# Sixteen instead of twelve contraction tiles of a down projection in a seven-product scheme

## The chip, the cores and the metric

The kernel runs on one core of a Trainium2 chip. The metric is the device time of one execution in microseconds; the time of a kernel is the median of several. Everything is computed in fp32. In this text PE is the matrix engine, PEld its weight loads, DVE the vector engine, ACT the scalar engine, POOL the GpSimd engine, and SP the engine that here only issues transfers.

## The reference

One layer of a hybrid encoder block on 512 tokens of 1024 channels. Shown is its frame; the three mixers (a bidirectional mLSTM, a neighbourhood attention and a cross attention) are left out, since the change does not touch them.

```python
def conv_glu_ffn(h, w_up, w_conv, b_conv, w_down):
    a, u = jnp.split(h @ w_up, 2, axis=-1)
    return (jax.nn.gelu(dwconv3(a, w_conv, b_conv)) * u) @ w_down

        x = x + merged @ w_out[l]
        x = x + conv_glu_ffn(rms_norm(x, ffn_norm_g[l]), w_ffn_up[l], w_ffn_conv[l], b_ffn_conv[l], w_ffn_down[l])
    return rms_norm(x, final_norm_g)
```

The last product, `@ w_down`, is the down projection: 512 tokens, a contraction over 2816 features, and 1024 columns out. Behind it come the residual sum and the final RMS norm.

## The kernel before

**Products.** Each fp32 operand is split into a high part (a rounded copy, formed by ACT) and a low part (the difference, formed by DVE). A product of two tiles is three matmuls into one sum: high by high, high by low, low by high (`mm3`, lines 195 to 198). A contraction tile is 128 features; a matmul takes a 128x128 block as its stationary side and streams 512 columns, or 256 near the end.

**The up projection.** For each of 22 feature tiles f two products run over the 8 tiles of the 1024 channels, `ua` and `uu`: 48 matmuls. Conv, gelu and the product with u follow on ACT and DVE while PE is in the next tile. The weights come through a ring of three raw buffers (`wr`, 512 KB each, SP's queue) and are split into rings of four tiles each (`wh`, `wl`; lines 178 and 179). The feature tiles f below 12 stay in fp32 (`uu_`), those from 12 on are split at once (`UH`, `UL`).

**The down projection by seven products.** Its first 2 * `WN` contraction tiles are done by the Strassen-Winograd scheme. Tokens are halved (256 each), so are the columns (512 each) and the contraction (`WN` tiles each). Instead of eight products of quarters there are seven, p1 to p7, each with `WN` tiles, 2 token tiles of 128 and 3 matmuls of 512 columns: 6 matmuls a tile. They need sums of quarters on both sides. The sums of the weights (T1 to T4) are formed by DVE under the up projection: `sum_load` (line 1254) loads four quarters of one tile as 1 MB into a buffer, four subtractions of 512 columns follow, and a store of 1 MB on POOL's queue puts them into `tdn`, a scratch in DRAM (line 1262). They are done three at a time, from f = 4 on. The sums of the tokens are formed by `ops_to` (line 1307) in front of each product, one half of a product's tiles (`GN` = `WN`/2) at a time: p5 takes a21 + a22 through a small scratch `s` (line 1325), p6 takes a22 - a21 after a21 has become a11 - a21 (lines 1334 and 1317), p3 takes a12 - a11 through the scratch (line 1327). The operand half is then split by ACT (line 1330) and DVE (line 1332) into a buffer of the pool `u`. The remaining `SN` contraction tiles are plain products: c0 for the left 512 columns, c1 for the right, 4 token tiles, 12 matmuls a tile.

**The order.** `SEGMENTS` gives the order of the products: p1, one tile of c0, p5, one of c0, p6, one of c0, p3, all of c1, two of c0, p7, p2, one of c0, p4, and at the end the last four tiles of c0. `raws_to`, `tiles_to` and `ops_to` load, split and form ahead by fixed distances: raw weights three pairs ahead, four split tiles, two or three operand halves. `todo` delays the additions of finished products by a few tiles. A scheduler puts the recorded instructions in order for each engine; each engine runs its list in order, and SP and POOL issue the transfers in order.

**Buffers.** The pool `u` has `NU` = 15 buffers of 2112 fp32 a partition. In the down projection five hold split u, four the fp32 u, two the residual with the half-done output, one the final norm's gain. Operand halves and every other pair of raw weights share the other three.

**The end.** The last four tiles of c0 are done token tile by token tile. A token tile's end is a sum with the residual (line 1499), a square with its sum on ACT (1418), a mean on DVE (1491), a power on POOL (1486), a scaling of the right half on ACT (1517) and of the left half on DVE (1518), and the store. The last token tile's four contraction tiles run in two halves of 256 columns, so that the first half's sum (1510) and square (1512) fall under the second; a small scalar (1515) carries the first half's square into the second's.

Of the kernel before, what the change touches and what calls it, by code (L numbers as in the profile page):

```python
# [11 lines left out]
F32 = mybir.dt.float32  # L12
# [93 lines left out]
def hybrid_block(ctx, tc, xg, xT, memT, wflat, wdn, wst, vecs, gbias, nabias, out):  # L106
# [1147 lines left out]
    def sum_load(k):  # L1254
# [5 lines left out]
        def store():  # L1260
# [3 lines left out]
        sums.extend([lambda: V.tensor_tensor(q[B11], q[B12], q[B11], op=ALU.subtract),  # L1264
                     lambda: V.tensor_tensor(q[B12], q[B22], q[B12], op=ALU.subtract),
# [16 lines left out]
    wraw, wsp, ops = {}, {}, {}  # L1282
    ahead = {"raw": 0, "tile": 0, "op": 0}
# [22 lines left out]

    def ops_to(n):
        while ahead["op"] < min(n, len(OPS)):
            name, g = OPS[ahead["op"]]
            v = [uu_[i][g][:, :GN * S].rearrange("p (k s) -> p k s", k=GN) for i in range(2)]  # L1310
            a11, a21, a12, a22 = v[0][:, :, :HS], v[0][:, :, HS:], v[1][:, :, :HS], v[1][:, :, HS:]
# [3 lines left out]
            srcs = [(0, GN, {"p1": a11, "p6": a11, "p7": a21, "p2": a12, "p4": a22}.get(name))]  # L1315
            if name == "p6":
                V.tensor_tensor(a11, a22, a21, op=ALU.subtract)
            elif srcs[0][2] is None:
                srcs = []
                for k in range(0, GN, 2):  # L1320
                    m = min(2, GN - k)
                    t = r3(scr(m * HS))
                    sl = slice(k, k + m)
                    if name == "p5":
                        V.tensor_tensor(t, a21[:, sl], a22[:, sl], op=ALU.add)
                    else:
                        V.tensor_tensor(t, a12[:, sl], a11[:, sl], op=ALU.subtract)
                    srcs.append((k, k + m, t))
            for i, j, src in srcs:
                A.activation(r3(h)[:, i:j], src, AF.Copy)  # L1330
            for i, j, src in srcs:
                V.tensor_tensor(r3(l)[:, i:j], src, r3(h)[:, i:j].bitcast(F32), op=ALU.subtract)
            if name == "p5":
                V.tensor_tensor(a21, a11, a21, op=ALU.subtract)
# [294 lines left out]
```

## Time and profile before

| | us |
|---|---|
| median of three runs (872.54 to 873.01) | 872.58 |
| profiled execution, its own time | 872.42 |
| its span in the trace | 870.6 |
| PE busy | 861.0 (99%) |
| DVE busy | 644.0 (74%) |
| ACT busy | 481.7 (55%) |
| first matmul of the down projection | at 747.08 |
| last matmul | at 862.72 |
| final operation on DVE | at 866.08 |

The granted clock of PE was 0.998 over the span. A row of a timeline gives the start, the duration, the engine, the line of the kernel, the operation with out<-in and the tile's shape; in brackets stands how long the engine had been idle before and what ended that. A name such as `wh` or `u` stands for all buffers of its ring; `at` and `mm` are sums in PSUM. Lines in the rows are those of the kernel before.

### The profile page before, as it was taken

The numbers are of one execution on the slowest core, as the hardware profiler recorded it, in microseconds if no ns is written. First come the engines' busy times: TensorE is split into PE (matmuls) and PEld (weight loads), VectorE is DVE, ScalarE is ACT, GpSimd is POOL, SyncE is SP. The second block draws the span as 40 slices with busy tenths as digits, with TensorE's granted clock in tenths as the row PEclk, the third lists the DMA queues.
The fourth block names the chain that finished last, engine by engine and source line by source line (L and its number), as shares of the span: only waits on it lengthen the run. The fifth ranks groups of instructions, "written<-read, shape, count | busy, mean of one in ns | idle before, by whom it ended". The sixth has DMA issues, their size and how long they took to land.

```text
span 870.6 us, 12096 instructions
## 1 busy us (share of the span) xinstructions
PE 861.0 (99%) x4176; PEld 723.3 (83%) x4176; DVE 644.0 (74%) x1365; ACT 481.7 (55%) x1003; POOL 87.2 (10%) x184
## 2 busy tenths in 40 slices
PE   9999999999999999999999999999999999999996
PEld 7898889888888888888888888888888888877885
DVE  7794698997477768897676659788667777984574
ACT  7563577764455658897534455444444444543353
POOL 0101100000343370600000000000000000000001
PEclk9999999999999999999999999999999999999999
DMA  8324642533343353533223434887222222456232
GB/s 276 100 75 147 196 141 85 173 107 112 96 132 88 107 145 112 159 119 122 97 97 110 145 109 145 292 288 242 80 97 99 96 98 95 154 167 218 61 120 97
DMA packets 43742, 117.50 MB, mean 135 GB/s; under 512 B 6041, under 2 KB 11161, under 8 KB 43681
## 3 DMA queue, kind: packets, MB, share of 16 engines
q1 hardware_dynamic: 34256, 103.73, 36.4%
q0 software_dynamic: 8992, 12.61, 5.3%
q8 instruction: 33, 0.54, 0.3%
q10 hardware_dynamic: 432, 0.39, 0.1%
q14 instruction: 29, 0.23, 0.1%
HBM read 106.20 MB, written 10.50 MB: 134 GB/s over the span
## 4 chain that ended last, share of the span: by engine, by line
PE 97%; DVE 1%; ACT 1%; issue 0%; DMA 0%; POOL 0%; POOLq 0%; ACTq 0%
PE mm L196 26%; PE mm L198 26%; PE mm L197 26%; PE at L197 4%; PE at L198 4%; PE at L196 4%; PE at L964 1%; PE at L945 1%; PE at L926 0%; PE at L927 0%; PE at L747 0%; PE at L795 0%; PE at L1052 0%; PE at L1244 0%; DVE u L1518 0%
## 5 line engine op out<-in xcount | busy, mean ns | idle before, releaser
L196 PE MATMUL mm<-u,wh 128*128 128x512 f32 (+1 forms) x907 | 353.6, 390 | 0.0
L198 PE MATMUL mm<-u,wl 128*128 128x512 f32 (+1 forms) x907 | 350.4, 387 | 0.0
L197 PE MATMUL mm<-u,wh 128*128 128x512 f32 (+1 forms) x907 | 350.1, 386 | 0.0
L178 ACT ACTIVATE wh<-wr 128x512 fp32r<-128x512 f32 (+1 forms) x256 | 159.9, 627 | 199.1 <-PE mm L197 158.2
L179 DVE TENSOR_TENSOR wl<-wr,wh 128x512 fp32r<-128x512 f32 (+2 forms) x258 | 175.5, 683 | 53.8 <-ACT wh L178 51.9
L198 PEld LDWEIGHTS mm<-u,wl 128*128 128x128 f32 x907 | 170.4, 188 | 34.7 <-DVE wl L179 0.2
L197 PEld LDWEIGHTS mm<-u,wh 128*128 128x128 f32 x907 | 170.7, 188 | 32.7
L196 PEld LDWEIGHTS mm<-u,wh 128*128 128x128 f32 x907 | 170.6, 188 | 32.8 <-ACT wh L178 0.4
L522 POOL DMA_DIRECT2D u<-nav_d x128 | 62.3, 511 | 70.6 <-DVE X L203 24.4
L197 PE MATMUL at<-wl,u 128*128 128x512 f32 (+2 forms) x172 | 60.0, 349 | 0.4 <-DVE wl L1303 0.3
L198 PE MATMUL at<-wh,u 128*128 128x512 f32 (+2 forms) x172 | 59.4, 346 | 0.0
L196 PE MATMUL at<-wh,u 128*128 128x512 f32 (+2 forms) x172 | 58.9, 348 | 0.4 <-ACT wh L1302 0.2
L197 PE MATMUL mm<-wl,u 128*128 128x512 f32 x108 | 42.2, 391 | 0.0
L198 PE MATMUL mm<-wh,u 128*128 128x512 f32 x108 | 42.1, 390 | 0.0
L196 PE MATMUL mm<-wh,u 128*128 128x512 f32 x108 | 41.6, 391 | 0.3 <-ACT wh L1302 0.3
L197 PEld LDWEIGHTS at<-wl,u 128*128 128x128 f32 x172 | 32.4, 188 | 6.2 <-DVE wl L1303 2.4
L196 PEld LDWEIGHTS at<-wh,u 128*128 128x128 f32 x172 | 32.1, 188 | 5.8 <-ACT wh L1302 2.1
L198 PEld LDWEIGHTS at<-wh,u 128*128 128x128 f32 x172 | 32.4, 189 | 3.8
L442 ACT ACTIVATE s<-pad,vec 128x512 f32<-128x512 f32 x30 | 24.4, 813 | 12.6 <-DVE pad L440 12.6
L1303 DVE TENSOR_TENSOR wl<-u,wh 128x512 fp32r<-128x512 f32 x30 | 20.1, 690 | 14.1 <-ACT wh L1302 14.0
L1302 ACT ACTIVATE wh<-u 128x512 fp32r<-128x512 f32 x30 | 18.2, 626 | 20.9 <-PE at L198 9.5
L1302 ACT ACTIVATE wh<-wr 128x512 fp32r<-128x512 f32 x32 | 19.6, 624 | 18.4 <-PE at L198 7.7
(338 smaller groups left out, 1126.6 us busy)
## 6 DMA issues: line engine op xcount, KB each, us to landing
wr<-wflat SPq DMA_DIRECT2D x125, 512.0 KB, 3.4
u<-wdn SPq DMA_DIRECT2D x6, 1024.0 KB, 7.6
tdn<-u POOLq DMA_DIRECT2D x6, 1024.0 KB, 5.5
nab<-nabias SPq DMA_DIRECT2D x16, 256.0 KB, 2.8
u<-nav_d POOLq DMA_DIRECT2D x128, 32.0 KB, 2.8
s<-xT SPq DMA_DIRECT2D x15, 256.0 KB, 3.8
u<-tdn SPq DMA_DIRECT2D x7, 512.0 KB, 3.9
wr<-wdn SPq DMA_DIRECT2D x5, 512.0 KB, 3.5
```

Source lines behind the costliest of these rows:

```text
L178: A.activation(h[:, u:v], src, AF.Copy)
L179: V.tensor_tensor(l[:, u:v], src, h[:, u:v].bitcast(F32), op=ALU.subtract)
L196: PE.matmul(ps, lh, rh, start=start, stop=False)
L197: PE.matmul(ps, lh, rl, start=False, stop=False)
L198: st["mm"] = PE.matmul(ps, ll, rh, start=False, stop=stop).ins
L442: A.activation(t1, pad[:, 0:512], AF.Identity, scale=vcol(w, i), bias=vcol(b, i))
L522: G.dma_start(vw[r * 32:(r + 1) * 32, i * 256:(i + 1) * 256], nav_v[hf, r, CW[b]:CW[b] + 32, hp * 256:(hp + 1) * 256])
L945: PE.transpose(pt[:, j * P:(j + 1) * P], sm[:, j * P:(j + 1) * P], ident)
L964: PE.matmul(py[:, bl * 256:(bl + 1) * 256], vw[:, c:c + P], pp[bl][:, hf * 256:(hf + 1) * 256], start=hf == 0, stop=hf == 1)
L1302: A.activation(h, src, AF.Copy)
L1303: V.tensor_tensor(l, src, h.bitcast(F32), op=ALU.subtract)
```

## The change

`WN` goes from 6 to 8, so that 16 of 22 contraction tiles go through the seven products and `SN` falls from 10 to 6. The rest follows from this or goes with it:

- The final segment of c0 is gone; p4 is the last. Its first two tiles run for both token tiles, the other six (`TK`) first for token tile 2 and then, in two halves of 256 columns, for token tile 3. The split weights of these six lie in three buffers of the pool `u` (`ends_w`) instead of the ring. Token tiles 0 and 1 are finished during p4 (`lead`, `finish`).
- Of the weight sums two subtractions of 512 columns become one of 1024. There are eight loads of 1 MB and eight stores instead of six.
- The token sums for p5 and p6 are formed in place by `early`, under the up projection, at f = 17 to 20, with the operand halves of p1 ahead of them. p3's two sums are formed in place in `ops_to`. No scratch is used, and the look-ahead is three halves throughout.
- The fp32 u still takes four buffers (now full), the split u three instead of five.

```diff
@@ -23,11 +23,10 @@
-WN = 6
+WN, TK = 8, 6
 SN = FT - 2 * WN
 SEGMENTS = (("p1", None), ("c0", (0,)), ("p5", None), ("c0", (1,)), ("p6", None), ("c0", (2,)), ("p3", None),
-            ("c1", range(SN)), ("c0", (3, 4)), ("p7", None), ("p2", None), ("c0", (5,)), ("p4", None),
-            ("c0", range(6, SN)))
+            ("c1", range(SN)), ("c0", (3, 4)), ("p7", None), ("p2", None), ("c0", (5,)), ("p4", None))
 NU = 15
@@ -1261,8 +1260,7 @@
-        sums.extend([lambda: V.tensor_tensor(q[B11], q[B12], q[B11], op=ALU.subtract),
-                     lambda: V.tensor_tensor(q[B12], q[B22], q[B12], op=ALU.subtract),
+        sums.extend([lambda: V.tensor_tensor(w[:, :2 * S], w[:, S:3 * S], w[:, :2 * S], op=ALU.subtract),
                      lambda: V.tensor_tensor(q[B22], q[B22], q[B11], op=ALU.subtract),
                      store])
@@ -1297,41 +1296,43 @@
             src = wraw.pop(TILES[ahead["tile"]])
-            h = wp.tile([P, HWT], F32R, tag="hi", name=nm("wh"), bufs=4)[:, :S]
-            l = wp.tile([P, HWT], F32R, tag="lo", name=nm("wl"), bufs=4)[:, :S]
+            i = ahead["tile"] - len(TILES) + TK
+            if i < 0:
+                h = wp.tile([P, HWT], F32R, tag="hi", name=nm("wh"), bufs=4)[:, :S]
+                l = wp.tile([P, HWT], F32R, tag="lo", name=nm("wl"), bufs=4)[:, :S]
+            else:
+                if i % 2 == 0:
+                    ends_w.append(unit(F32R))
+                h, l = [ends_w[-1][:, o * S:(o + 1) * S] for o in (i % 2, 2 + i % 2)]
...
+    def early(g, i):
+        a11, a21, a12, a22 = quarters(g)
+        if i == 0:
+            V.tensor_tensor(a21, a21, a22, op=ALU.add)
+        else:
+            V.tensor_tensor(a11, a21, a11, op=ALU.subtract)
...
-            srcs = [(0, GN, {"p1": a11, "p6": a11, "p7": a21, "p2": a12, "p4": a22}.get(name))]
-            if name == "p6":
-                V.tensor_tensor(a11, a22, a21, op=ALU.subtract)
-            elif srcs[0][2] is None:
-                srcs = []
-                for k in range(0, GN, 2):
-                    m = min(2, GN - k)
-                    t = r3(scr(m * HS))
-                    sl = slice(k, k + m)
-                    if name == "p5":
-                        V.tensor_tensor(t, a21[:, sl], a22[:, sl], op=ALU.add)
-                    else:
-                        V.tensor_tensor(t, a12[:, sl], a11[:, sl], op=ALU.subtract)
-                    srcs.append((k, k + m, t))
-            for i, j, src in srcs:
-                A.activation(r3(h)[:, i:j], src, AF.Copy)
-            for i, j, src in srcs:
-                V.tensor_tensor(r3(l)[:, i:j], src, r3(h)[:, i:j].bitcast(F32), op=ALU.subtract)
-            if name == "p5":
-                V.tensor_tensor(a21, a11, a21, op=ALU.subtract)
+            if name == "p3":
+                V.tensor_tensor(a21, a22, a11, op=ALU.subtract)
+                V.tensor_tensor(a11, a12, a11, op=ALU.subtract)
+            src = {"p1": a11, "p5": a21, "p6": a11, "p3": a11, "p7": a21, "p2": a12, "p4": a22}[name]
+            A.activation(r3(h), src, AF.Copy)
+            V.tensor_tensor(r3(l), src, r3(h).bitcast(F32), op=ALU.subtract)
@@ -1388,8 +1389,14 @@
-        if f == FT - 4:
-            ops_to(1)
+        i = f - 2 * WN
+        if 1 <= i < 5:
+            g = (i - 1) // 2
+            if i % 2:
+                ops_to(g + 1)
+                early(g, 0)
+            else:
+                early(g, 1)
@@ -1440,87 +1446,95 @@
+    def lead(t):
+        V.tensor_tensor(xt[t][:, :S], A4[t], xt[t][:, :S], op=ALU.add)
+        squares(t, part[t], 0, S)
+
+    def finish(t):
+        x, col = xt[t], power(mean(part[t]))
+        A.activation(x[:, S:], x[:, S:], AF.Copy, scale=col)
+        V.scalar_tensor_tensor(x[:, :S], x[:, :S], col, gfin[:, :S], op0=ALU.mult, op1=ALU.mult)
+        SY.dma_start(out[t * P:(t + 1) * P, :], x)
...
             if ks is None and k % GN == 0:
-                ops_to(OPS.index((name, k // GN)) + (2 if j == 0 else 3))
+                ops_to(OPS.index((name, k // GN)) + 3)
...
+            if name == "p4":
+                if k < WN - TK:
+                    for t in range(2):
+                        wino(name, A4[2:], k, t, full, False, t == 1 and k == WN - TK - 1)
...
+                    plain(name, k, t, A4[t], full, k == 0, t < 2 and k == SN - 1)
+                if k == SN - 1:
+                    later(2, lambda: (lead(0), lead(1)))
+                    later(4, lambda: (finish(0), finish(1)))
+
+    x = xt[3]
+    V.tensor_tensor(x[:, :S], A4[3], x[:, :S], op=ALU.add)
+    tk = range(WN - TK, WN)
+    for k in tk:
+        wino("p4", A4[2:], k, 0, full, False, k == WN - 1)
+    lead(2)
+    z, ends = unit(), [atps(), atps()]
+    for e in range(2):
+        cs = slice(e * HS, (e + 1) * HS)
+        for k in tk:
+            wino("p4", [None, ends[e][:, :HS]], k, 1, cs, k == tk[0], k == WN - 1)
+        if e == 0:
+            finish(2)
+        V.tensor_tensor(z[:, cs], ends[e][:, :HS], x[:, cs], op=ALU.add)
...
```

Up to the feed-forward stage the instructions stand as before on every engine. In the following rows a name's last number tells the buffers apart. First ACT around the operand halves of p6; before, `u_1420_7610` and `u_1432_7654` are these two halves, and the `wh` rows between them are splits of weight tiles:

```order
L1330 ACTIVATE u_1406_7548<-s_1408_7551 128x256
L1302 ACTIVATE wh_1417_7592<-wr_1411_7568 128x512
L1408 ACTIVATE s_1431_7645<-at_1397_7509 128x512
L1302 ACTIVATE wh_1421_7614<-wr_1411_7568 128x512
L1330 ACTIVATE u_1420_7610<-u_1048_5547 128x768
L1302 ACTIVATE wh_1425_7626<-u_1416_7590 128x512
L1302 ACTIVATE wh_1428_7638<-u_1416_7590 128x512
L1302 ACTIVATE wh_1433_7658<-wr_1419_7608 128x512
L1330 ACTIVATE u_1432_7654<-u_1098_5818 128x768
L1302 ACTIVATE wh_1436_7670<-u_1427_7636 128x512
```

And with the change, where they are `u_1421_7618` and `u_1436_7673`:

```order
L1334 ACTIVATE u_1421_7618<-u_1048_5547 128x1024
L1415 ACTIVATE s_1432_7652<-at_1398_7512 128x512
L1307 ACTIVATE wh_1422_7621<-u_1412_7576 128x512
L1307 ACTIVATE wh_1426_7633<-wr_1417_7598 128x512
L1307 ACTIVATE wh_1429_7645<-wr_1417_7598 128x512
L1307 ACTIVATE wh_1433_7661<-u_1420_7616 128x512
L1334 ACTIVATE u_1436_7673<-u_1114_5908 128x1024
L1307 ACTIVATE wh_1437_7676<-u_1420_7616 128x512
```

A half is now 1024 columns wide and comes with four weight tiles' splits between it and the next one instead of three. Second, DVE under the up projection of f = 17 with the change, where neither of the two wide rows stood before (L178 splits a weight tile of the up projection, L1335 is the low part of an operand half of p1, L1321 the first sum in place):

```order
L178 TENSOR_TENSOR wl_1322_7109<-wr_1306_7022,wh_1321_7108 128x512
L1335 TENSOR_TENSOR u_1326_7144<-u_1048_5547,u_1326_7144 128x1024
L439 TENSOR_TENSOR pad1_140<-mm_1317_7070,rb_2_5625 128x512
L178 TENSOR_TENSOR wl_1324_7113<-wr_1306_7022,wh_1323_7112 128x512
L1321 TENSOR_TENSOR u_1048_5547<-u_1048_5547 128x4x256
L442 SCALAR_TENSOR_TENSOR s_1318_7096<-pad1_140,vec_78,s_1318_7096 128x512
L178 TENSOR_TENSOR wl_1330_7152<-wr_1312_7060,wh_1329_7151 128x512
```

Each wide row stands between two rows that PE's weight loads or the conv depend on. Third, the end on DVE, before and with the change (`at` of 256 columns are the two halves of the last token tile, and `u_1384_7487` or `u_1385_7490` is the final gain):

```order
L1499 TENSOR_TENSOR u_1047_5545<-mm_1387_7491,u_1047_5545 128x512
L1510 TENSOR_TENSOR u_1597_8430<-at_1583_8359,u_1047_5545 128x256
L1491 TENSOR_SCALAR y_1595_8423<-y_1560_8258,y_1593_8420 128x1
L1518 SCALAR_TENSOR_TENSOR u_1047_5545<-u_1047_5545,y_1596_8425,u_1384_7487 128x512
L1491 TENSOR_SCALAR y_1600_8447<-y_1562_8262,y_1598_8444 128x1
L1510 TENSOR_TENSOR u_1597_8430<-at_1584_8360,u_1047_5545 128x256
L1515 SCALAR_TENSOR_TENSOR u_1597_8430<-y_1600_8447,y_1601_8449 128x1
L1518 SCALAR_TENSOR_TENSOR u_1047_5545<-u_1597_8430,y_1604_8468,u_1384_7487 128x512
```

```order
L1515 TENSOR_TENSOR u_1047_5545<-mm_1389_7495,u_1047_5545 128x512
L1461 TENSOR_TENSOR u_1047_5545<-mm_1388_7494,u_1047_5545 128x512
L1457 TENSOR_SCALAR y_1594_8421<-y_1567_8276,y_1589_8397 128x1
L1467 SCALAR_TENSOR_TENSOR u_1047_5545<-u_1047_5545,y_1595_8423,u_1385_7490 128x512
L1527 TENSOR_TENSOR u_1591_8400<-at_1592_8401,u_1047_5545 128x256
L1457 TENSOR_SCALAR y_1598_8432<-y_1569_8280,y_1596_8429 128x1
L1532 SCALAR_TENSOR_TENSOR u_1591_8400<-y_1598_8432,y_1599_8434 128x1
L1527 TENSOR_TENSOR u_1591_8400<-at_1593_8402,u_1047_5545 128x256
L1535 SCALAR_TENSOR_TENSOR u_1047_5545<-u_1591_8400,y_1602_8459,u_1385_7490 128x512
```

The scaling of the token tile before (L1518, now L1467) stood between the two halves' sums and now stands ahead of both; the small scalar (L1515, now L1532) stood behind the second sum and now stands ahead of it.

More of the change, by code (lines that the diff above doesn't have):

```diff
@@ L1426, in half_done, with wino @@
             V.tensor_tensor(xt[t][:, S:], xt[t][:, S:], gfin[:, S:], op=ALU.mult)
-    def wino(name, ps, k, start, stop):
+    def wino(name, ps, k, t, cs, start, stop):
         g, kk = divmod(k, GN)
@@ L1431, in wino @@
         wh, wl = wsp[name, k]
-        for t in range(2):
-            q = slice(kk * HS + t * P, kk * HS + (t + 1) * P)
-            mm3(ps[t], h[:, q], l[:, q], wh, wl, start, stop or t == 1 and name == "p4" and k == WN - 1)
+        q = slice(kk * HS + t * P, kk * HS + (t + 1) * P)
+        mm3(ps[t], h[:, q], l[:, q], wh[:, cs], wl[:, cs], start, stop)
     def plain(name, k, t, ps, cs, start, stop):
@@ new lines, in hybrid_block @@
+    x = xt[3]
[12 more added lines that the diff above has]
+        V.tensor_tensor(z[:, cs], ends[e][:, :HS], x[:, cs], op=ALU.add)
+        v = tiny(1)
+        A.activation(scr(HS + e), z[:, e * HS:(e + 1) * HS + e], AF.Square, scale=D ** -0.5, accum_out=v)
+        if e == 0:
+            v = mean((part[3][0], v))
+            V.scalar_tensor_tensor(z[:, S:S + 1], v, D ** 0.5, power(v), op0=ALU.mult, op1=ALU.mult)
```

110 lines of the change are left out of this document (41 added, 69 removed).

## The prediction

> **What bounds the kernel now.** I read the page first, then the chain of waits, then TensorE by stages, and last the waits inside the stage that the change rewrites.
>
> ```profile
> span 870.6 us, 12096 instructions
> PE 861.0 (99%) x4176; PEld 723.3 (83%) x4176; DVE 644.0 (74%) x1365; ACT 481.7 (55%) x1003; POOL 87.2 (10%) x184
> PE 97%; DVE 1%; ACT 1%; issue 0%; DMA 0%; POOL 0%; POOLq 0%; ACTq 0%
> ```
>
> TensorE (PE) is the bound: busy in 99% of the span, 97% of the chain. A change can then act in three ways: the number of matmuls, the gaps between them, and the end behind the last. For the first I need the distance between starts, from PE's timeline (start, duration; a duration overlaps the next start):
>
> ```profile
> 719.88 0.39 PE L196 MATMUL mm<-u,wh 128*128 128x512 f32 x1
> ...
> 723.28 0.39 PE L196 MATMUL mm<-u,wh 128*128 128x512 f32 x1
> ...
> 747.08 0.39 PE L196 MATMUL at<-wh,u 128*128 128x512 f32 x1
> ...
> 859.97 0.28 PE L196 MATMUL at<-wh,u 128*128 128x256 f32 x1
> ...
> 862.72 0.28 PE L198 MATMUL at<-wh,u 128*128 128x256 f32 x1
> ```
>
> Between the first two rows lie 15 steps: 3.40/15 = 0.2267 us for 512 columns. Between the last two lie 23: 2.75/23 = 0.1196 us for 256. The down projection begins at 747.08 and its stream ends at 862.72 + 0.12 = 862.84, after 115.76 us. The order counts 480 matmuls of 512 columns and 24 of 256 in it: 480 x 0.2267 + 24 x 0.1196 = 111.68. So **4.08 us** of this stage are gaps. Busy time by stretches says where (columns: PE, PEld, DVE, ACT, POOL, clock, DMA share, GB/s):
>
> ```profile
> 747.08:755.24 8.16, 8.16 (x38) 6.76 (x37) 8.16 (x15) 6.51 (x12) 0.00 (x0) 1.00 0.55 169
> 755.24:791.00 35.76, 34.61 (x141) 25.43 (x140) 30.69 (x51) 17.56 (x32) 0.00 (x0) 1.00 0.53 160
> 791.00:855.00 64.00, 64.00 (x284) 53.00 (x284) 36.31 (x55) 26.33 (x45) 0.00 (x0) 1.00 0.36 117
> ```
>
> Only 755 to 791 shows idle PE (1.15 us; in the rest of the 4.08 PE counts as busy, since a matmul's duration covers part of each gap). That is the run through p5, p6 and p3. The table of waits (total, times, longest) for ACT from 747 to 792 and for the weight loads:
>
> ```profile
> ACT u L1330 <- PE at L198: 15.3, 5, 3.6
> PEld at L197 <- DVE wl L1303: 2.4, 5, 0.8
> PEld at L196 <- ACT wh L1302: 2.1, 4, 0.6
> ```
>
> PE's weight loads wait for wh and wl, the split weight tiles. Why these are late stands in one piece of the timelines:
>
> ```profile
> 756.17 0.96 DVE L1334 TENSOR_TENSOR u<-u 128x768 f32<-128x768 f32 x1
> 756.31 0.19 PEld L197 LDWEIGHTS mm<-wl,u 128*128 128x128 f32 x1 [0.43 <-DVE wl L1303]
> 762.68 0.85 ACT L1330 ACTIVATE u<-u 128x768 fp32r<-128x768 f32 x1 [3.58 <-PE at L198]
> 763.43 1.13 ACT L1302 ACTIVATE wh<-u 128x512 fp32r<-128x512 f32 x2
> 764.09 0.30 PEld L196 LDWEIGHTS at<-wh,u 128*128 128x128 f32 x2 [0.52 <-ACT wh L1302]
> ```
>
> There are two causes. First, at 762.68 the copy of an operand half (L1330) has stood 3.58 us at the head of ACT's queue, until PE was done with the half whose buffer it takes; behind it, at 763.43, stands the split of the next weight tile, which PE needs six matmuls = 1.36 us after the release. That pattern comes five times. Second, up to 756 DVE is full with the sums of tokens (8.16 of 8.16 us in the first stretch), and wl waits behind them.
>
> **The change part by part.** *Matmuls.* The order has 462 + 36 now, 18 long ones fewer and 12 short ones more: -18 x 0.2267 + 12 x 0.1196 = **-2.64 us**. The Trainium skill (TensorE: Matmul & The Clock Gate, "Back-to-back issue gap") gives N/2.4 + 2.5 ns for an isolated matmul, 215.8 and 109.2 ns here; by it the term were -2.57. The rows decide.
>
> *Gaps.* Of the 15 buffers of this pool, three were left for operand halves and raw weights (12 hold the up projection's result, the residual and a gain); now five are. In the new order the halves of p6 and p3 take buffers whose last reader is done by the time that the ring of four split tiles lets ACT go on anyway; one, the second half of p6, still waits for the end of p5's first half, but the tile behind it is due 18 matmuls = 4.1 us later instead of 1.36. The p5 and p6 sums leave this stage. What remains costs, by these rows (out<-in, count, busy, mean ns, idle):
>
> ```profile
> L1303 DVE TENSOR_TENSOR wl<-u,wh 128x512 fp32r<-128x512 f32 x30 | 20.1, 690 | 14.1 <-ACT wh L1302 14.0
> L1330 ACT ACTIVATE u<-u 128x768 fp32r<-128x768 f32 x10 | 8.4, 843 | 12.1 <-PE at L198 9.6 <-DVE wl L1303 2.3
> L1332 DVE TENSOR_TENSOR u<-u,u 128x768 fp32r<-128x768 f32 x10 | 9.6, 958 | 5.7 <-ACT u L1330 5.5
> ```
>
> 256 columns more cost DVE 958 - 690 = 268 ns, so 1024 columns are 1.23 us (an estimate, like the next figures). A half of four weight tiles is 24 matmuls = 5.44 us of PE against 4 x 0.69 + 1.23 = 3.99 us of DVE. From p1 to the end of p3 the order puts 49 instructions of 512 and 11 of 1024 columns on DVE: 49 x 0.69 + 11 x 1.23 = 47.3 us at most against 228 matmuls = 51.7 us, 92%; before, 8.16 + 30.69 = 38.85 of 43.92, 88%. That is no lighter; but the sums now stand where nothing waits for them. Walking the rows of DVE and ACT with these durations (a successor starts about 0.1 before the listed end), each weight tile is ready a microsecond or more ahead, tightest at p5's last tile. Bounds: all gaps go, **-4.08**, or all stay, 0. I take -4.08, since both causes are removed by name, and keep 0 for the range.
>
> *Up projection.* One 1 MB load, one 1 MB store and four 512-wide subtractions come for each of two more tiles; at f = 17 and 19 one operand half and a sum (two 1024-wide, 2.5 us), at f = 18 and 20 one sum. The rows for single feature tiles, and the stores:
>
> ```profile
> 559.37:570.73 11.36, 11.36 (x55) 9.41 (x53) 11.36 (x20) 4.76 (x8) 1.08 (x2) 1.00 0.82 292
> 570.73:582.10 11.37, 11.37 (x55) 9.41 (x53) 10.88 (x18) 5.51 (x9) 1.21 (x2) 1.00 0.90 320
> 627.10:638.00 10.90, 10.90 (x50) 9.04 (x49) 7.38 (x11) 4.61 (x8) 0.00 (x0) 1.00 0.31 96
> L1262 POOL DMA_DIRECT2D tdn<-u x6: 752/753/797, 547.9 to 600.1; - x6
> ```
>
> PE did not idle with DVE full for a whole tile, nor at 320 GB/s. Each tile with a sum now moves 3 x 1.05 MB in 11.36 us = 277 GB/s, no more than was seen, over two tiles more. At f = 17 DVE has 7.38 + 2.5 = 9.9 of 10.9 us. So I take **0** under this cover; uncovered, the eight subtractions (4.8 us at the listed pace of 0.60 each) and the six pieces of 1024 columns (6 x 1.23 = 7.4) would cost up to 12 us. The Trainium skill (SBUF — State Buffer, "Who interferes with whom") says that a DVE operation with two SBUF inputs contends with GpSimd's reads, and that descriptors of a queue that GpSimd writes can starve. That speaks against two more stores on POOL's queue under such subtractions; but the stores' rows read 752 to 797 ns beside a full DVE, so the trace shows no holding, and I leave the term at 0.
>
> *End.* The rows of DVE and ACT behind the last long matmuls:
>
> ```profile
> 854.73 0.69 DVE L1499 TENSOR_TENSOR u<-mm,u 128x512 f32<-128x512 f32 x1 [1.36 <-PE mm L198]
> 857.11 0.75 DVE L1518 SCALAR_TENSOR_TENSOR u<-u,y,u 128x512 f32<-128x512 f32 x1 [0.69 <-POOL y L1486]
> 857.78 0.68 DVE L1499 TENSOR_TENSOR u<-mm,u 128x512 f32<-128x512 f32 x1
> 861.60 0.42 DVE L1510 TENSOR_TENSOR u<-at,u 128x256 f32<-128x256 f32 x1
> 862.46 0.19 ACT L1512 ACTIVATION_READ_ACCUMULATOR s<-u 128x1 f32 x1
> 863.14 0.75 DVE L1518 SCALAR_TENSOR_TENSOR u<-u,y,u 128x512 f32<-128x512 f32 x1 [0.65 <-POOL y L1486]
> 863.81 0.21 DVE L1491 TENSOR_SCALAR y<-y,y 128x1 f32<-128x1 f32 x1
> 863.94 0.42 DVE L1510 TENSOR_TENSOR u<-at,u 128x256 f32<-128x256 f32 x1
> 864.67 0.16 DVE L1515 SCALAR_TENSOR_TENSOR u<-y,y 128x1 f32<-128x1 f32 x1 [0.32 <-POOL y L1486]
> 864.92 0.42 ACT L1512 ACTIVATE s<-u 128x257 f32<-128x257 f32 x1 [1.06 <-DVE u L1515]
> 866.08 0.75 DVE L1518 SCALAR_TENSOR_TENSOR u<-u,y,u 128x512 f32<-128x512 f32 x1 [1.25 <-POOL y L1486]
> ```
>
> Now the final operation of the last token tile starts 866.08 - 862.84 = 3.24 us behind the stream. One reason: the last matmul's record ends at 862.72 + 0.28 = 863.00, but its sum starts at 863.94, because DVE first finishes the token tile before (863.14) and a mean (863.81). In the new order the halves last 36 x 0.1196 = 4.31 us from a point T, so more of the tile before falls under them. With steps from the rows: sum of that tile at about T + 0.2 (estimate: a record runs 0.16 past the next start), its last operation 857.11 - 854.73 = 2.38 later, first half's sum 857.78 - 857.11 = 0.67 later (T + 3.25), its square summed at 862.65 - 861.60 = 1.05 later (T + 4.30), the scalar of L1515 864.67 - 863.81 = 0.86 later (T + 5.16), second half's sum 0.13 later (T + 5.29), its square 0.46 later, the final operation 866.08 - 864.92 = 1.16 later: T + 6.91, 2.60 us behind the stream. **-0.64 us**; at best the second sum waits for nothing and the final operation comes 0.16 + 0.46 + 1.16 = 1.78 behind (-1.46), at worst nothing is won (0).
>
> *Sum*, against the profiled execution's own 872.42 us (median of the runs 872.58): 872.42 - 2.64 - 4.08 - 0.64 = **865.06**, say 865.1.
>
> **The rivals.** *The gaps stay.* For it: DVE is as full as before in this run (92% by the high durations), p6's second half still waits, and p5's last tile has only a microsecond. Against it: the queue behind each wait is now long. A step that is later than my walk by over 1 us decides. All gaps kept give 872.42 - 2.64 - 0.64 = 869.1, half of them 867.1.
>
> *Transfers become the bound, and it is slower.* Seven products need a new 0.262 MB weight tile each six matmuls: 0.262 MB/1.36 us = 193 GB/s, and the stretch of products is longer now. These rows bear on it (a window, and the issue of one load with its time to landing):
>
> ```profile
> 790.00:800.00 10.00, 10.00 (x46) 8.27 (x45) 4.87 (x8) 3.27 (x5) 0.00 (x0) 1.00 0.88 290
> u<-tdn SPq DMA_DIRECT2D x7, 512.0 KB, 3.9
> ```
>
> One load at a time would be 0.524 MB/3.9 us = 134 GB/s, and 755 to 791 ran at 160. If 160 were a limit, the 35 tiles up to p3's end (9.17 MB) would take 57.3 instead of 51.7 us, and the 25 of p7, p2, p4 and c0 (6.55 MB) 41.0 instead of 35.4: +11.2, so 865.1 + 11.2 = 876.3. It is slower than before once the rate stays under 15.72 MB/(87.1 + 7.4 us) = 166 GB/s. Against it: 290 GB/s in 790 to 800 with PE full, and the low rate of 160 stood where PE itself was waiting for ACT and DVE.
>
> *The up projection shows what it hides.* If each of the eight tiles with sums overran by the added 0.6 us of DVE: 8 x 0.6 = 4.8, 869.9. Against it: only two of these tiles filled DVE, and the weights are three loads ahead.
>
> That the change does not do what it says is out: the order has six matmuls fewer and the sums where they should be.
>
> **How the numbers follow.** Forecast (864.0 to 866.2) 0.62; gaps stay, half or more, 0.22; up projection 0.05; transfers 0.06, a third of it mild and still faster; something else 0.05, either way. The range reaches over the kept gaps: 863.9 to 869.2, leaving out about 0.15. What tells from no change is 0.2%, 1.7 us. Faster takes the first three cases, the mild transfers and half of the rest: 0.62 + 0.22 + 0.05 + 0.02 + 0.02 = 0.93, cut to 0.92; same 0.03; slower 0.05.
>
> **What would show it.** In the new profile: 462 and 36 matmuls from about 747 on, ending 109.04 us later (462 x 0.2267 + 36 x 0.1196), with PE's share of each stretch at its full width; the weight loads' waits for wh and wl at L1307 and L1308 under 0.5 us in sum; the waits of L1334 for PE shorter; the down projection's start still at 747.1, else the up projection has paid; the final operation some 2.6 us behind the last matmul. Waits of L1307 for a DMA would speak for the transfers, waits of weight loads for wl alone for a DVE that is too full. A time above 869.2 would make my walk of the rows wrong, one above 872 the whole reading.

## The result and the profile after

The changed kernel takes 865.38 us in the median (865.00 to 865.74) against 872.62 us; the ratio is 0.9916, with an interval of 0.9899 to 0.9933. The profiled execution took 865.0 us, 7.42 us less than the one before, and the page of the changed kernel reads (first lines, and the chain by engine):

```profile
span 863.2 us, 12105 instructions
PE 855.3 (99%) x4170; PEld 722.1 (84%) x4170; DVE 653.6 (76%) x1359; ACT 487.2 (56%) x1001; POOL 88.8 (10%) x186
...
PE 99%; DVE 0%; ACT 0%; POOL 0%; POOLq 0%; issue 0%
```

PE is still the bound, and the chain now has hardly anything else in it. The down projection on PE's timeline, its first matmul, the first of the 36 halves and the last:

```profile
746.88 0.39 PE L195 MATMUL at<-wh,u 128*128 128x512 f32 x1
...
851.60 0.28 PE L195 MATMUL at<-u,u 128*128 128x256 f32 x1
...
855.79 0.28 PE L197 MATMUL at<-u,u 128*128 128x256 f32 x1
```

From 746.88 to 855.79 + 0.12 = 855.91 are 109.03 us. The matmuls alone are 462 x 0.2267 + 36 x 0.1196 = 109.04. Nothing is left for gaps, and the table of waits for the weight loads is empty from 440 us on. The busy time by stretches shows the same, with DVE as full as before or fuller and with more transfer (PE, PEld, DVE, ACT, POOL, clock, DMA share, GB/s):

```profile
747.00:755.00 8.00, 8.00 (x37) 6.64 (x36) 8.00 (x13) 5.59 (x9) 0.00 (x0) 1.00 0.66 197
755.00:791.00 36.00, 36.00 (x160) 29.80 (x160) 30.80 (x44) 21.29 (x32) 0.00 (x0) 1.00 0.65 206
791.00:852.00 61.00, 61.00 (x273) 50.55 (x272) 41.30 (x63) 30.30 (x54) 1.10 (x2) 1.00 0.42 135
```

ACT still waits for PE, but in small pieces, and at another instruction (the two largest rows for it from 747 to 792, and the one for an operand half):

```profile
ACT wh L1307 <- PE at L197: 10.1, 15, 0.7
ACT wh L1307 <- PE mm L197: 2.8, 3, 1.1
...
ACT u L1334 <- PE at L197: 0.7, 1, 0.7
```

Fifteen times it is the weight split itself that waits for its ring of four, which is what a loop that runs ahead looks like; an operand half waits once for PE, for 0.7 instead of five times for 15.3 us in sum. The end on DVE:

```profile
851.80 0.69 DVE L1461 TENSOR_TENSOR u<-mm,u 128x512 f32<-128x512 f32 x1 [2.61 <-PE mm L197]
...
854.15 0.75 DVE L1467 SCALAR_TENSOR_TENSOR u<-u,y,u 128x512 f32<-128x512 f32 x1 [0.65 <-POOL y L1452]
854.81 0.42 DVE L1527 TENSOR_TENSOR u<-at,u 128x256 f32<-128x256 f32 x1
...
856.67 0.16 DVE L1532 SCALAR_TENSOR_TENSOR u<-y,y 128x1 f32<-128x1 f32 x1 [0.65 <-POOL y L1452]
856.75 0.42 DVE L1527 TENSOR_TENSOR u<-at,u 128x256 f32<-128x256 f32 x1
858.43 0.75 DVE L1535 SCALAR_TENSOR_TENSOR u<-u,y,u 128x512 f32<-128x512 f32 x1 [1.26 <-POOL y L1452]
```

The final operation starts 858.43 - 855.91 = 2.52 us behind the stream, before 3.24. So the 7.42 us come from the stage's length (115.76 to 109.03: -6.73), its end (-0.72), a start that is 0.20 earlier, a stretch behind the final operation that is 0.25 longer (4.52 to 4.77 us), and 0.02 outside the span. The start lies between 746.88 and 747.65 in all runs here that leave the mixers' buffers alone, so the 0.20 is no effect of the change that I could claim.

### The profile page after: what moved, and what is told of

Its sections match the earlier page's. It is cut to its first block, busy times and chain, and to the rows that moved or that the text cites. A ratio compares the mean times of both kernels' runs of the same rounds, so it can differ in the third digit from the quotient of the medians.

```text
span 863.2 us, 12105 instructions
## 1 busy us (share of the span) xinstructions
PE 855.3 (99%) x4170; PEld 722.1 (84%) x4170; DVE 653.6 (76%) x1359; ACT 487.2 (56%) x1001; POOL 88.8 (10%) x186
## 4 chain that ended last, share of the span: by engine, by line
PE 99%; DVE 0%; ACT 0%; POOL 0%; POOLq 0%; issue 0%
PE mm L195 26%; PE mm L197 26%; PE mm L196 26%; PE at L195 5%; PE at L197 5%; PE at L196 5%; PE at L963 1%; PE at L944 1%; PE at L925 0%; PE at L926 0%; PE at L746 0%; PE at L794 0%; PE at L1243 0%; PE at L1051 0%; PE at L224 0%; PE mm L403 0%
## 5 line engine op out<-in xcount | busy, mean ns | idle before, releaser
L178 DVE TENSOR_TENSOR wl<-wr,wh 128x512 fp32r<-128x512 f32 (+2 forms) x258 | 175.6, 684 | 56.9 <-ACT wh L177 54.9
L197 PE MATMUL mm<-wh,u 128*128 128x512 f32 x92 | 35.8, 389 | 0.0
L196 PE MATMUL mm<-wl,u 128*128 128x512 f32 x92 | 35.8, 389 | 0.0
L195 PE MATMUL mm<-wh,u 128*128 128x512 f32 x92 | 35.7, 389 | 0.0
L1261 POOL DMA_DIRECT2D tdn<-u x8 | 6.1, 762 | 252.5 <-DVE u L1260 252.5
L1308 DVE TENSOR_TENSOR wl<-wr,wh 128x512 fp32r<-128x512 f32 x34 | 23.2, 689 | 8.8 <-ACT wh L1307 8.7
```

The costliest lines, as they stand in the source:

```text
L178: V.tensor_tensor(l[:, u:v], src, h[:, u:v].bitcast(F32), op=ALU.subtract)
L195: PE.matmul(ps, lh, rh, start=start, stop=False)
L196: PE.matmul(ps, lh, rl, start=False, stop=False)
L197: st["mm"] = PE.matmul(ps, ll, rh, start=False, stop=stop).ins
L1261: G.dma_start(tdn[:, :, k * S:(k + 1) * S].rearrange("q p n -> p q n"), w4)
L1308: V.tensor_tensor(l, src, h.bitcast(F32), op=ALU.subtract)
```

## The experiments

The question was no longer how much, but why the gaps went. The prediction named two causes: too few free buffers for operand halves, and sums of tokens that fill DVE in the down projection. In the following, the length of the stream is read from PE's timeline as above, and its gaps are that length less the matmuls at 0.2267 and 0.1196 us. "Late" and "early" say where the sums stand in the program. Where DVE ran them is another matter, since the scheduler orders the instructions: "in the stage" counts, by the trace, how many of the four sums (two halves of p5, two of p6) DVE ran with the down projection and not under the up projection. Through the scratch the first of them starts 0.27 us ahead of the stage's first matmul and is counted.

| kernel | tiles | free buffers | sums for p5, p6 | in the stage | stream | matmuls | gaps | median us |
|---|---|---|---|---|---|---|---|---|
| before | 12 | 3 | late, through scratch | 4 | 115.76 | 111.68 | 4.08 | 872.6 |
| changed | 16 | 5 | early, in place | 0 | 109.03 | 109.04 | 0 | 865.38 |
| late sums | 16 | 5 | late, in place | 1 | 109.10 | 109.04 | 0.06 | 865.40 |
| one held | 16 | 4 | early, in place | 0 | 109.29 | 109.04 | 0.25 | 865.72 |
| two held | 16 | 3 | early, in place | 0 | 113.87 | 109.04 | 4.83 | 870.13 |
| 13 throughout | 16 | 3 | early, in place | 1 | 114.62 | 109.04 | 5.58 | 880.80 |
| 13 and late sums | 16 | 3 | late, in place | 1 | 113.26 | 109.04 | 4.22 | 878.79 |
| twelve, early | 12 | 3 | early, in place | 0 | 113.03 | 111.76 | 1.27 | 869.53 |
| twelve, late | 12 | 3 | late, in place | 1 | 112.81 | 111.76 | 1.05 | 869.26 |
| old, in place | 12 | 3 | late, in place | 1 | 113.22 | 111.68 | 1.54 | 870.24 |
| old, in place, pieces | 12 | 3 | late, in place, cut | 1 | 112.64 | 111.68 | 0.96 | 869.26 |
| four tiles at the end | 16 | 5 | early, in place | 0 | 108.96 | 108.97 | 0 | 865.72 |
| eight tiles at the end | 16 | 5 | early, in place | 0 | 109.11 | 109.12 | 0 | 864.65 |
| new end only | 12 | 3 | late, through scratch | 4 | 116.09 | 111.76 | 4.33 | 872.13 |

### Thirteen buffers

```diff
-NU = 15
+NU = 13
```

> The changed kernel with 13 instead of 15 buffers in the pool u, so that three instead of five are left for operand halves and raw weights, as before the change; the early sums stay. Buffers as the main cause of the gaps (my reading): the halves' copies wait for PE again with a weight tile behind them; of the 4.08 us some 2.8 stood in waits for wh, so 2 to 4 us come back, 867.4 to 869.4, with weight loads waiting for wh. Rival, the sums of tokens alone were the cause: the time stays at 865.4 within 0.4, no waits of weight loads. A down projection that begins later than 746.9 would mean that the missing buffers hurt under the up projection instead.

Measured: 880.80 us, ratio 1.0092 (1.0073 to 1.0111), far outside both expectations, and the last sentence of mine says where to look. The first and the last matmul of its down projection:

```profile
756.86 0.39 PE L195 MATMUL at<-wh,u 128*128 128x512 f32 x1
...
871.36 0.28 PE L197 MATMUL at<-u,u 128*128 128x256 f32 x1
```

The stage begins 10 us late: the pool serves the whole kernel, and with 13 buffers PE waits in the mixers, too (by the waits up to 450 us, among others 2.8 us for the state C that DVE forms in line 724 and 2.0 for the loads of the window attention). That part says nothing on the change. The stage itself is 114.62 us long, 5.58 of them gaps. The experiment was too coarse, and the two runs with held buffers below replace it.

### The sums late again

```diff
-        i = f - 2 * WN
-        if 1 <= i < 5:
...
+        if f == FT - 4:
+            ops_to(1)
...
+            if name in ("p5", "p6"):
+                early(g, int(name == "p6"))
...
-                ops_to(OPS.index((name, k // GN)) + 3)
+                ops_to(OPS.index((name, k // GN)) + (2 if j == 0 else 3))
```

> The changed kernel with the sums for p5 and p6 formed again in front of their products (in place, 1024 columns wide) instead of under the up projection; 15 buffers, five of them free. My reading: four sums of 1.23 us return to DVE in its first 25 us, where it was full before; weight loads wait for wl, and 0.5 to 2 us come back, 865.9 to 867.4, all of it between 745 and 770. Rival, buffers alone were the cause: 865.4 within 0.4, no waits.

Measured: 865.40 us, ratio 0.9919 (0.9904 to 0.9934), the same as the changed kernel. The expectation was of four sums back in the stage, but **the edit moved them in the program and only one of them on the engine.** DVE's four rows for the sums of p5 (L1319) and p6 (L1321) start at 640.80, 684.32, 721.52 and 748.89; in the changed kernel they start at 640.70, 684.23, 699.58 and 721.35. So the scheduler left three of the four under the up projection, although the program now has them behind it. (In the changed kernel, too, they do not run where `early` stands: PE is in the tiles f = 12 to 19 at these times, and the L1321 that was shown at f = 17, as the first sum in place, is a sum for p6; p5's are L1319.) The rows of DVE between 748 and 754 show the one sum that is back, and the table of waits for the weight loads has one row:

```profile
748.89 1.22 DVE L1321 TENSOR_TENSOR u<-u 128x1024 f32<-128x1024 f32 x1
750.02 0.69 DVE L1373 TENSOR_TENSOR s<-s,rb 128x512 f32<-128x512 f32 x1
750.63 0.68 DVE L1308 TENSOR_TENSOR wl<-wr,wh 128x512 fp32r<-128x512 f32 x1
...
753.63 2.35 DVE L1337 TENSOR_TENSOR u<-u,u 128x1024 fp32r<-128x1024 f32 x2
```

```profile
PEld at L196 <- DVE wl L1308: 0.2, 1, 0.2
```

DVE is as full as in the changed kernel (busy 9.67 of 10 us from 745 to 755, there 9.74), and PE does not mind: wl is split so far ahead that 2.35 us of operand work in front of it cost 0.2. One sum in the stage costs 0.06 us with five buffers free; what four would cost there, which was the question, this run does not show.

### Both undone

The two edits above in one kernel.

> Both undone: late sums and 13 buffers, only the sixteen tiles and the new end kept. If both causes are real and add up: 3 to 6 us, 868.4 to 871.4. If one alone is the cause: the same time as the run that undoes that one. If neither is: 865.4.

Measured: 878.79 us, ratio 1.0077 (1.0061 to 1.0092); the stage begins at 755.68 and has 4.22 us of gaps, 1.4 less than with early sums. But in either kernel DVE ran one of the four sums in the stage (L1321 at 762.27 here, at 756.95 with early sums), so the pair says little of the sums; that two kernels with the same work can differ by 1.4 us is what it does say.

### Two buffers held, one buffer held

```diff
+    held = [unit() for _ in range(2)]
+    for d in held:
+        V.memset(d[:, :1], 0.0)
     gfin = unit()[:, :D]
...
     A.dma_start(out[3 * P:, S:], x[:, S:])
+    for d in held:
+        V.tensor_scalar(tiny(1), d[:, :1], 1.0, None, op0=ALU.add)
```

The second run has `range(1)` in the first line.

> The changed kernel with two of the five free buffers held from the end of the up projection to the end of the program (one column is written at the start and read at the end, which is all that is added), so that the mixers keep their 15 buffers and only the down projection has three free. With 13 buffers throughout the down projection took 114.6 instead of 109.0 us. Buffers as the cause: the start stays at 746.9 and 4 to 6 us of gaps come back, 869.4 to 871.4. Rival, the lost time of the run with 13 buffers came from what the delayed mixers left behind: 865.4 to 866.5.

> The same with one buffer held, four free. Buffers as a cause that grows with each one missing: 1 to 3 us, 866.4 to 868.4. If four are enough: 865.4 within 0.4.

Measured with two held: 870.13 us, ratio 0.9969 (0.9957 to 0.9980), start at 747.02, 4.83 us of gaps. With one held: 865.72 us, ratio 0.9919 (0.9902 to 0.9935), 0.25 us of gaps. Four buffers are all but enough, three are not; my "1 to 3 us for one" was wrong, the cost does not grow evenly. What PE's weight loads and ACT wait for with two held (ACT from 747 to 792):

```profile
PEld at L195 <- ACT wh L1307: 3.0, 4, 1.1
PEld at L196 <- DVE wl L1308: 2.1, 5, 0.5
```

```profile
ACT wh L1307 <- DMA u<-tdn: 6.7, 4, 4.2
ACT wh L1307 <- DMA u<-wst: 5.9, 2, 4.0
ACT u L1334 <- PE at L197: 4.5, 2, 2.3
```

The operand halves wait for PE again, and beside them appears a wait that the kernel before hardly had: ACT stands up to 4.2 us at a raw weight's transfer. Halves and every other raw pair share the buffers, so a short ring delays both; that the load goes out late because its buffer comes free late, and not because the transfer is slow, I infer from the changed kernel, where the same loads at 206 GB/s let ACT wait for 0.2 us. SP's rows fit: the first four loads `u<-tdn` go out at 758.09, 764.79, 770.65 and 776.78 with two held, at 752.51, 755.94, 762.18 and 769.07 in the changed kernel. In both kernels all four sums run ahead of the stage, so here nothing but the buffers differs.

### Twelve tiles with the new sums and the new end

```diff
-WN, TK = 8, 6
+WN, TK = 6, 6
...
-            ("c1", range(SN)), ("c0", (3, 4)), ("p7", None), ("p2", None), ("c0", (5,)), ("p4", None))
+            ("c1", range(SN)), ("c0", (3, 4)), ("p7", None), ("p2", None), ("c0", range(5, SN)), ("p4", None))
...
-                    plain(name, k, t, A4[t], full, k == 0, t < 2 and k == SN - 1)
+                    plain(name, k, t, A4[t], full, k == 0, t != 2 and k == SN - 1)
```

> Twelve contraction tiles as before, but with the early sums and the new end (p4 last; 474 matmuls of 512 columns and 36 of 256); three buffers free as before, since five hold split u. Matmuls: 12 more long ones than the changed kernel, 12 x 0.2267 = 2.72, so 868.1 without gaps. My reading: the buffers' gaps stay, 2 to 3 us more, 870 to 871. Rival, the sums were the cause: 868.1 within 0.5 and no waits for wh.

The second kernel has the late sums of above in addition.

> Twelve contraction tiles with the new end, three free buffers, and the sums for p5 and p6 late again and in place. The twelve tiles with early sums took 869.5, 1.3 us of gaps against 4.1 in the kernel before. If the early sums are what closed 2.8 of it: 871.5 to 872.5. If it was something else that both share (the new end, sums in place instead of through the scratch): 869.5 within 0.5.

Measured: 869.53 us, ratio 0.9965 (0.9954 to 0.9977), and 869.26 us, 0.9961 (0.9946 to 0.9976). The first lies between my reading and its rival and bears out neither. Early or late in the program is the same again. But both have only 1.27 and 1.05 us of gaps with three free buffers, where the kernel before has 4.08: something that both share had closed about 3 us, and the number of buffers cannot be it. Both share the new end and the form of the sums, and by the trace the place of three sums, too: with late sums those for p5 start at 607.88 and 641.36 and the first for p6 at 720.40, under the up projection, and only the second for p6, at 756.53, in the stage. The next two runs part the end from the sums.

### The form of the sums, and the end, each alone

The first is the kernel before with the sums in place:

```diff
-            srcs = [(0, GN, {"p1": a11, "p6": a11, "p7": a21, "p2": a12, "p4": a22}.get(name))]
...
+            if name == "p5":
+                V.tensor_tensor(a21, a21, a22, op=ALU.add)
+            elif name == "p6":
+                V.tensor_tensor(a11, a21, a11, op=ALU.subtract)
+            elif name == "p3":
+                V.tensor_tensor(a21, a22, a11, op=ALU.subtract)
+                V.tensor_tensor(a11, a12, a11, op=ALU.subtract)
...
```

> The kernel before, twelve tiles and its old end, with one edit: the sums for p5, p6 and p3 in place, each one instruction of 768 columns, instead of through the scratch in pieces of 512 and 256; they stay where they were in the program, and three buffers are free. If the form of the sums closed the 3 us of gaps that the twelve-tile runs lack: 869.4 to 870.2, and no waits of weight loads before 770. If the new end did: 872.6 within 0.4.

The second is the twelve-tile kernel with late sums, whose sums go through the scratch again as in the kernel before.

> The other half: twelve tiles, the new end, late sums through the scratch in pieces as in the kernel before. If the form of the sums is the cause: the gaps of 4.1 us are back, the end is 0.7 us shorter and the halves cost 0.08 more, 872.0 within 0.5. If the new end moved the buffers' turns and so closed the gaps: 869.3 within 0.5.

Measured: 870.24 us, ratio 0.9969 (0.9956 to 0.9982), gaps 1.54; and 872.13 us, ratio 0.9992 (0.9983 to 1.0002), gaps 4.33. So it is the edit of the sums, and not the new end. The second kernel repeats even the waits of the kernel before, among them the row of an operand half:

```profile
ACT u L1345 <- PE at L197: 15.3, 5, 3.6
```

What the edit did in the first, DVE's and SP's rows tell. The sums did not stay where they stand in the program: without the scratch those for p5 start at 608.10 and 641.40 and the first for p6 at 720.43, where the kernel before has the first at 746.81; and a third sum of each half, behind p5's before (L1334), now stands in front of p3's. The split of the low parts of two weight tiles (`wl<-u`) had stood behind these sums and now runs earlier, and so does the load that takes the buffer which this split frees (SP waited 2.6 us for it before). Rows of DVE, SP and ACT, before:

```profile
756.17 0.96 DVE L1334 TENSOR_TENSOR u<-u 128x768 f32<-128x768 f32 x1
757.03 1.03 DVE L1332 TENSOR_TENSOR u<-s,u 128x512 fp32r<-128x512 f32 x2
757.98 1.29 DVE L1303 TENSOR_TENSOR wl<-u,wh 128x512 fp32r<-128x512 f32 x2
759.34 0.32 SPq L1292 DMA_DIRECT2D u<-tdn  x1
...
769.71 1.16 ACT L1302 ACTIVATE wh<-u 128x512 fp32r<-128x512 f32 x2 [0.90 <-DMA u<-tdn]
```

With the sums in place:

```profile
754.17 0.68 DVE L1303 TENSOR_TENSOR wl<-wr,wh 128x512 fp32r<-128x512 f32 x1
754.77 1.28 DVE L1303 TENSOR_TENSOR wl<-u,wh 128x512 fp32r<-128x512 f32 x2
756.09 0.32 SPq L1292 DMA_DIRECT2D u<-tdn  x1
760.89 1.15 ACT L1302 ACTIVATE wh<-u 128x512 fp32r<-128x512 f32 x2 [1.60 <-DMA u<-tdn]
762.74 0.85 ACT L1323 ACTIVATE u<-u 128x768 fp32r<-128x768 f32 x1 [0.69 <-PE at L198]
763.49 0.61 ACT L1302 ACTIVATE wh<-wr 128x512 fp32r<-128x512 f32 x1
```

The operand half is copied at nearly the same time (762.74, before 762.68), since PE releases its buffer then; but two weight splits that stood behind it now stand ahead of it. They could not have stood there before. Their load, out at 759.34 instead of 756.09, landed 3.7 us later, at about 763.0, and the splits began at 763.43: the half at the head of ACT's queue, where it had stood for 3.58 us, held them up by 0.4 us of that at most. At the next half, the row at 769.71, they waited for their load even after the half was copied. So in the kernel before the load was late, too, and it was late because one of the three shared buffers came free late, behind sums on DVE.

### In place, but in pieces

The edit "in place" also replaced pieces of 512 and 256 columns by one of 768. So the last run cuts the in-place sums of p5 and p3 and their halves into the same pieces:

```diff
+            cuts = [slice(k, min(k + 2, GN)) for k in range(0, GN, 2)] if name in ("p5", "p3") else [slice(0, GN)]
             if name == "p5":
-                V.tensor_tensor(a21, a21, a22, op=ALU.add)
+                for c in cuts:
+                    V.tensor_tensor(a21[:, c], a21[:, c], a22[:, c], op=ALU.add)
...
```

> The kernel before with the sums in place as in the run on the form of the sums (870.2), but for p5 and p3 cut again into pieces of 512 and 256 columns, and their operand halves too. If the number of instructions that DVE and ACT carry is what the 2.5 us of gaps hung on, they return: 872.0 to 872.8. If it was the way through the scratch: 870.2 within 0.5, with weight loads waiting from 774 on only.

Measured: 869.26 us, ratio 0.9958 (0.9941 to 0.9975), gaps 0.96. That is 0.4 us below the lower of the two expected ranges, and the weight loads wait from 774 on only, as expected. It has as many sums and copies as the kernel before, in the same sizes, and the gaps stay closed. So neither the number nor the size of the instructions brings them back. It does not follow that the way through the scratch is the cause by itself: here, too, the sums for p5 run from 599.52 to 641.40 and the first for p6 at 720.45, ahead of the stage, and ACT has the same order as in the run without pieces (the two splits from 760.89, the half at 762.74). Without the scratch the sums leave the stage, the load goes out earlier and the order on ACT changes, all in one, and these runs cannot part the three: none has the scratch with the sums ahead of the stage, and none has all four sums in place within it. Why the scheduler left the sums in the stage with the scratch is open.

### Four or eight tiles for the halves

```diff
-WN, TK = 8, 6
+WN, TK = 8, 4
```

> The changed kernel with four tiles of p4 held for the end instead of six. The chain from the start of the halves to the final operation was 6.83 us with six; if it sets the end, it stays, and the halves last 24 x 0.1196 = 2.87, so the final operation comes 3.96 us behind the stream instead of 2.52; matmuls 0.07 less: 1.4 us slower, 866.8. If the end hangs on the last half alone: 865.3.

```diff
-WN, TK = 8, 6
+WN, TK = 8, 8
...
-                    plain(name, k, t, A4[t], full, k == 0, t < 2 and k == SN - 1)
+                    plain(name, k, t, A4[t], full, k == 0, t != 2 and k == SN - 1)
```

> The changed kernel with all eight instead of six tiles of p4 held for the end, so that the two halves of the last token tile last 48 x 0.1196 = 5.74 us instead of 4.31. My reading of the end: the second half's sum then waits only for its matmuls, the final operation comes 0.16 + 0.46 + 1.23 = 1.85 us behind the stream instead of 2.52; two tiles of 512 columns turned into halves add 12 x 0.1196 - 6 x 0.2267 = 0.07: 0.6 us faster than the changed kernel, 864.8. Rival, the end is set by the chain behind the last matmul alone: no change, 865.4; and four instead of three buffers for these weights could bring gaps in p2 and p4, 866 or more.

Measured: four tiles 865.72 us, ratio 0.9919 (0.9904 to 0.9935); eight tiles **864.65 us**, ratio 0.9909 (0.9895 to 0.9924), the fastest of all by its median, though its interval overlaps that of the changed kernel. In the run with eight the last matmul starts at 856.21, and DVE's rows are:

```profile
855.66 0.16 DVE L1532 SCALAR_TENSOR_TENSOR u<-y,y 128x1 f32<-128x1 f32 x1 [0.65 <-POOL y L1452]
856.53 0.42 DVE L1527 TENSOR_TENSOR u<-at,u 128x256 f32<-128x256 f32 x1 [0.71 <-PE at L197]
858.21 0.75 DVE L1535 SCALAR_TENSOR_TENSOR u<-u,y,u 128x512 f32<-128x512 f32 x1 [1.25 <-POOL y L1452]
```

The small scalar is done before the last half's sum, which waits for PE alone; the final operation comes 858.21 - 856.33 = 1.88 us behind the stream (1.85 expected), against 2.52. Nothing but matmuls is left ahead of that sum. With four tiles the last matmul starts at 856.16, and I was wrong, since the scheduler put the first half's sum ahead of the token tile before:

```profile
855.04 0.42 DVE L1527 TENSOR_TENSOR u<-at,u 128x256 f32<-128x256 f32 x1 [0.74 <-PE at L197]
...
856.23 0.75 DVE L1467 SCALAR_TENSOR_TENSOR u<-u,y,u 128x512 f32<-128x512 f32 x1 [0.65 <-POOL y L1452]
...
859.18 0.75 DVE L1535 SCALAR_TENSOR_TENSOR u<-u,y,u 128x512 f32<-128x512 f32 x1 [1.26 <-POOL y L1452]
```

That is 859.18 - 856.28 = 2.90 us behind, not 3.96: the order on DVE was another with each of the three sizes, and a chain that is walked in one order need not hold in the next.

## Why the prediction was right, and what of its reason stays open

- **Matmuls, -2.64.** Right, term and total: the stage's 109.03 us are the 109.04 of the count. The Trainium skill (TensorE: Matmul & The Clock Gate, "Back-to-back issue gap") states its formula for an isolated matmul; by it the stage would be 462 x 0.2158 + 36 x 0.1092 = 103.6 us, an estimate. This case's trace, without a single wait of a weight load in it, does not agree and decides.
- **Gaps, -4.08.** Right in size; of the two causes, one is shown in part and one is open.
  - *Too few buffers*: shown for sixteen tiles by the held buffers, 0, 0.25 and 4.83 us with five, four and three free. Of the 4.08 us in the kernel before it is not the whole: with three buffers still, taking the scratch away closed all but 1.54 (0.96 when cut into pieces). What more buffers would do to that kernel was not tried. The copy that had stood 3.58 us at the head of ACT's queue, the row on which this cause rested, held up the splits behind it by 0.4 at most, since their load had not landed earlier.
  - *The sums leave this stage*: neither refuted nor shown by itself. The "late" runs, meant to undo it, put one sum of four back, for 0.06 us with sixteen tiles and nothing with twelve. The two kernels with all four sums in the stage, both with the scratch, have 4.08 and 4.33 us of gaps; every run with less than 2 has at least three of them ahead of it. The rows fit this cause, wl behind sums, but by a longer way than I had seen: the late wl also kept the buffer for the next load.
  - So the -4.08 came true with a bundle: two more buffers, and an edit that took the scratch away and let the sums run ahead of the stage, for p5 and p6 even ahead of their place in the program. I had given the scratch no price, and that all of the gaps went was in part luck.
- **Up projection, 0.** Right, though the sums ran at other tiles than f = 17 to 20. No weight load waits from 440 us to the start of the down projection. Two stretches of the busy time in the changed kernel, the fullest with transfers and the one with the last sums of weights, and the row of the eight stores:

```profile
581.90:593.20 11.30, 11.30 (x54) 9.35 (x52) 9.13 (x14) 4.49 (x8) 0.00 (x0) 1.00 0.86 322
616.00:627.00 11.00, 11.00 (x52) 9.12 (x51) 10.15 (x16) 5.38 (x9) 1.50 (x2) 1.00 0.74 237
```

```profile
L1261 POOL DMA_DIRECT2D tdn<-u x8: 752/754/797, 547.9 to 622.4; - x8
```

  PE was full at 322 GB/s, and the eight stores took 752 to 797 ns each. What the Trainium skill (SBUF — State Buffer, "Who interferes with whom") says of GpSimd starving beside DVE shows nowhere here, which fits its note, marked there as inferred, that tensor_tensor takes only the reading side of the shared ports.
- **End, -0.64.** Measured -0.72. Each step of the walk came within 0.15 us (T = 851.60; first half's sum at T + 3.21 for 3.25, scalar of L1532 at T + 5.07 for 5.16, final operation at T + 6.83 for 6.91). The reading that DVE's order, not the last matmul, sets the end is borne out by the run with eight tiles.
- **Rivals.** The gaps' staying is what the kernel would have done with three buffers: 870.13, near the 869.1 written for it. The transfers ran at 206 GB/s, above the 193 that the products need, with no wait of PE and one of 0.2 us of ACT, so 160 was no limit of the transfers.

## What to carry to other kernels

In this kernel a ring that was one buffer short cost little and two short much; so count who shares a ring and hold single buffers to find the edge, rather than to cut the pool. A full engine is not a cause: DVE was full at the start of the down projection before (8.16 of 8.16 us) and with the change (8.00 of 8.00), and only before did PE's weight loads wait behind it; ask what stands behind what. Where a scheduler sets the order, an edit to the program's order is not yet one to the engine's: look in the trace at where the moved work ran before reading the time as its price. And an edit that adds no work (a scratch less) can let work run earlier and change who stands at the head of a queue; compare the orders before pricing it at nothing.

## What was not expected of the hardware and the kernel

A 512 KB load of weight sums into the shared buffers took 4.6 us to land in the median in the changed kernel instead of 3.9, at 206 instead of 160 GB/s from 755 to 791, without PE noticing. Beyond that nothing of the hardware: each surprise was an order of instructions or the sharing of a pool, most of all the sums that ran far ahead of their place in the program, and the 10 us that the stages ahead of the down projection lose with 13 buffers.
